# A two-layer streaming encoder step: the delta rule's decay matrices, its rows of exp and all parts of the first output weight are made in the first projection stage and read back from DRAM

## The chip, the core and the metric

The kernel runs on one core of one Trainium2 chip. The metric is the time of one launch on the device in microseconds (us), as the median of the runs; less is better. One further execution was taken by the hardware profiler, and all rows of views below come from that one. The engines are PE (TensorE), ACT (ScalarE), DVE (VectorE), POOL (GpSimd) and SP (SyncE, which here issues most DMAs).

## The reference

2048 prompt tokens and 32 sample tokens (2080 rows of 1024 values, all float32) pass one gated delta layer, a shared K/V projection and one sliding-window attention layer. The change touches the delta layer:

```python
proj = x @ w_in                                  # q, k, v, gate z, and two small columns a, b
qkv  = silu(causal_conv(proj[..., :CONV_DIM]))   # 4 taps; q and k are then l2-normalised
g    = -exp(a_log) * softplus(a_in + dt_bias);  beta = sigmoid(b_in)
# in blocks of c positions, 8 heads:
gcum  = cumsum(g)
decay = exp(where(incl, gcum[:, None] - gcum[None, :], -inf))
lower = where(strict, (k*beta) @ k.T * decay, 0)
u, w  = solve(lower + I, v*beta), solve(lower + I, k*beta*exp(gcum))
intra = q @ k.T * decay
v_new = u - w @ S;   o = (q*exp(gcum)) @ S + intra @ v_new
S     = S * exp(gcum[-1]) + (k*exp(gcum[-1]-gcum)).T @ v_new
out   = (rmsnorm(o) * silu(z)) @ w_out           # then residual and layer norm
```

The kernel uses blocks of 128 positions: 17 tiles, of which tile 0 holds the 32 sample rows (with a state of its own) and tiles 1 to 16 the prompt.

## The kernel before

**Precision.** The large products are made of float32 values split in a high and a low part (`w_hi`, `w_lo`, `act_hi`, `act_lo`), three matmuls each (L77 to L79). The split of a weight is an ACT cast and a POOL or DVE subtraction.

**Order.** The tile framework puts each engine's instructions in an order by an estimate of its own, except where the program switches to an order written out by hand: PE and DVE in the gate stage, and PE, DVE and ACT in the delta loop. SP's queue and POOL's are ordered by the framework throughout, so a DMA need not stand where the program calls for it.

**P1, `P1.qkv`.** The input stays in SBUF as five blocks of 416 rows. First come the small columns, out of which `gates` makes `gcum` for all tiles; it turns each tile's 128 values of 8 heads on PE (L379), copies them on DVE (L381) into one of two row buffers and stores them to the scratch `gcum` from ACT's queue (L382). Then 24 heads (8 of q, 8 of k, 8 of v) follow: PE projects 5 blocks, ACT copies them out of PSUM (L227, six banks in turn), ACT and DVE do the convolution and the SiLU over the whole row of 2083 values (L194, L196, L199, L200), for q and k also the sums of squares (L207 to L210), and SP stores the head (L202). `fetch_weights` (L46) asks for the weight of a later head as soon as its only raw buffer is free. In heads 15 to 22 `split_out_weights` splits the first half of the output weight of the delta layer, a piece of 128 x 512 each, in the buffer that the tanh (`th`) uses, and keeps the parts in the scratch `wo`. After the last head of k, `norms` finishes the factors per token, the bias `ngc` of the decays among them.

**Gate stage.** PE projects the gate z for three of the five blocks; beside it `Ahead` prepares the triangular inverses of tiles 0 and 1.

**Delta loop, `Delta.run`.** Turn i finishes tile i, inverts tile i+1, begins tile i+2 and loads for tile i+3. `decays` makes E, 128 x (8 x 128): DVE adds the mask `nm` to the rows `gb` that were read with broadcast from `gcum` (L542), ACT takes exp with the bias `ngc` (8 times, L547). There is one buffer for E. `lower` multiplies k k^T (PE, L562) by E (DVE, L563) and turns the diagonal blocks into `L` (L572); POOL runs 25 steps of a substitution on it (`chain`: L585 and L588), DVE the rest. `inside` multiplies q k^T (PE, L629) by E (L630). `powers` takes exp of `gb` itself (ACT, L638), and `fade` multiplies k and q by it (DVE, L646). `turn_v` and `turn_k` turn v (PE, L612) and k (L598) on PE. `emit` multiplies the output by the gate and stores it (L800) out of the buffer that the gate was read into; v and z share three buffers of half a tile (L531 loads them). Up to turn 10 (`OPEN` is 11) pieces of the gate projection of the last two blocks fill PE between the steps. Then the left half of SBUF is given to `O1`, the output projection with layer norm, whose tiles fill PE in the last turns. It needs the whole output weight in two parts; `load_part_weights` reads four of the eight pairs from `wo` (L1050, L1051), and four raw weights (L1047), which ACT casts (L1059) and DVE subtracts (L1063), a step at a time in turns 11 to 14.

**Afterwards**: the second layer's projections, the attention and its output projection, which the change does not touch.

Of the kernel before, what the change touches and what calls it, by code (L numbers as in the profile page):

```python
# [26 lines left out]
H = 8  # L27
# [63 lines left out]
def drain(gen):  # L91
    for _ in gen:
        pass


class P1:
# [49 lines left out]
    def qkv(self):  # L146
# [180 lines left out]
def gates(nc, I, T, G, abT, gtmp, one, pt):  # L327
# [135 lines left out]
class Delta:  # L463
# [36 lines left out]
    def constants(self):  # L500
        nc, one = self.nc, self.one
        self.nm = one.tile([128, 128], F32, tag="nm", name="nm")
        nc.sync.dma_start(self.nm[:], self.I["nm"])
        self.tinit = one.tile([128, 32, 8], F32, tag="tinit", name="tinit")
        nc.sync.dma_start(self.tinit[:], self.I["tinit"])
# [5 lines left out]
    def load(self, ch, name, halves=(0, 1)):  # L511
# [25 lines left out]
    def decays(self, ch):  # L537

        nc, V, G = self.nc, self.nc.vector, self.G
        n, ti = ch.n, ch.ti  # L540
        ch.E = self.two.tile([128, 8, 128], F32, tag="E", name="E", bufs=1)
        V.tensor_tensor(out=ch.E[:n, :, :n], in0=ch.gb[:n, :, :n],  # L542
                        in1=self.nm[:n, :n].unsqueeze(1).to_broadcast([n, 8, n]), op=ALU.add)
        yield
        for h in range(8):
            E = ch.E[:n, h, :n]
            nc.scalar.activation(E, E, AF.Exp, bias=G["ngc"][:n, ti, h:h + 1])  # L547
            if h % 4 == 3:
                yield

# [68 lines left out]
    def inside(self, ch):  # L619
# [3 lines left out]
        for q in range(2):  # L623
# [8 lines left out]
            yield  # L632

    def powers(self, ch):

        for hs in (slice(0, 4), slice(4, 8)):
            eg = ch.gb[:, hs, :ch.n]
            self.nc.scalar.activation(eg, eg, AF.Exp)  # L638
        yield

# [162 lines left out]
    def run(self, chunks, S, first, second, side, done):  # L803
# [7 lines left out]
        def go(*gens):  # L811
            for g in gens:
                next(g, None)
# [6 lines left out]
        fill = first.give  # L820
        drain(self.decays(c0))
        side(False)
# [4 lines left out]
        fill(1.0)  # L827
        k, w, g, d, low = self.turn_k(c0), self.turn_v(c0), self.inside(c0), self.decays(c1), self.lower(c1)
        for s, us in ((w, 0.6), (k, 0.6), (w, 0.6), (k, 0.6), (g, 0.6), (g, 0.6), (d, 0.0), (d, 0.0), (d, 1.2), (d, 1.2),
                      (low, 1.2), (low, 1.2)):  # L830
            go(s)
            fill(us)
        drain(self.powers(c0))
        drain(self.fade(c0))
# [6 lines left out]
        drain(self.powers(c1))  # L841
        drain(self.decays(c2))
        self.S, S = S, self.S
# [4 lines left out]
        for i in range(len(chunks) + 1):  # L848
# [32 lines left out]
            go(a, t, a, t, seen, sq)  # L881
            go(gen(self.powers, n2))
            side(0)
# [25 lines left out]
            fill(2 * more + 2 * gate)  # L909
            d = gen(self.decays, n3)  # L910
            go(v)
            fill(gate)
            go(r, g, r, r, r, r, v, r, k, r, d)
            if i > self.OPEN:
# [18 lines left out]
            fill(more)  # L933
            go(v, o, d, d)
            side(1)
# [26 lines left out]
class Ahead(Delta):  # L962
# [13 lines left out]
    def inverses(self, chunks):  # L976

        tmps = []
        for ch in chunks:
            tmp = Chunk(ch.t0, ch.n)  # L980
            own = ch if ch.pool else tmp
            for name in ("gb", "k"):
                self.load(own, name)
            tmp.gb, tmp.k = own.gb, own.k
            tmps.append(tmp)
        yield
        for name in ("q", "v"):
            self.load(chunks[0], name)
        for ch, tmp in zip(chunks, tmps):
            yield from self.decays(tmp)  # L990
# [46 lines left out]

def load_part_weights(nc, pool, stage, src, kept, sub):


    hi, lo = (pool.tile([128, KC, D], F32R, tag=n, name=n) for n in ("wo_hi", "wo_lo"))
    m = kept.shape[1]
    raws = {}

    def load(k):
        raws[k] = stage.tile([128, D], F32, tag="r", name="wo_raw")
        nc.sync.dma_start(raws[k][:], src[k])  # L1047

    def fetch(k, q):
        q.dma_start(hi[:, k, :].bitcast(F32), kept[0, k])  # L1050
        q.dma_start(lo[:, k, :].bitcast(F32), kept[1, k])  # L1051

    yield hi, lo
    load(m)
    load(m + 1)
    fetch(0, nc.sync)
    yield
    for k in range(m, KC):
        nc.scalar.copy(hi[:, k, :], raws[k][:])  # L1059
        if k - m + 1 < m:  # L1060
            fetch(k - m + 1, nc.scalar)
        yield
        sub.tensor_tensor(out=lo[:, k, :], in0=raws[k][:], in1=hi[:, k, :], op=ALU.subtract)  # L1063
        if k + 2 < KC:
            load(k + 2)
        yield
# [37 lines left out]
class OutNorm:  # L1104


    def __init__(self, tc, es, name, side, I, pre, banks, kept):
        self.nc = nc = tc.nc
        self.one = new_pool(tc, es, name + "_one", 1, side=side)
        self.two = new_pool(tc, es, name + "_two", 2, side=side)  # L1110
        self.pp = new_pool(tc, es, name + "_pp", banks, PSUM, side=side)
        self.tabs = None
        self.tables = lambda: ln_tables(nc, self.one, I[pre + "_ln_g"], I[pre + "_ln_b"])
        self.rest = load_part_weights(nc, self.one, self.two, I[pre + "_w_out"], kept, nc.vector)
        self.w = next(self.rest)
# [637 lines left out]
def host_inputs(inp):  # L1753
# [56 lines left out]
    "z": (NTT, 128, 8, 128),  # L1810
    "wo": (2, 4, 128, D),
    "wob": (2, KC, 128, D),
    "gcum": (NTT, 8, 128),
    "o": (NS, 8, 128),
    "g": (NTT, 128, 8, 128),
# [49 lines left out]
```

## Time and profile before

| what | value |
|---|---|
| median of 3 runs | 2196.88 us (2190.58 to 2197.76) |
| the profiled execution | 2196.05 us, its span 2194.3 us |
| busy PE / DVE / ACT / POOL | 2149.0 / 1373.7 / 917.6 / 841.7 us |
| mean granted PE clock | 0.991 |
| moved by DMA | 274.48 MB, mean 125 GB/s |
| P1 and gate stage / delta loop / rest | about 0 to 705 / 705 to 1150 / 1150 to 2194 us |

The rows of the views have this form. In a group: line, engine, operation, output<-input, size, count | busy us in all, mean ns of one | idle us before them and what ended it. In a timeline: start us, length us, engine, line, operation [idle before it <-what ended it]. In a table of stretches: busy us and instructions of PE, of its weight loads, of DVE, ACT and POOL, then the granted PE clock, the share of the DMA engines and GB/s. A "q" behind an engine's name is its sequencer, which issues DMAs.

### The profile page before, as it was taken

The page shows a single profiled execution, that of the slowest core. Times are in us where ns is not written, and L with a number is a line of the kernel's source. Part 1 is how long each engine was busy: PE and PEld are TensorE (multiplying, and loading weights), DVE is VectorE, ACT ScalarE, POOL GpSimd, SP SyncE. Part 2 cuts the span into 40 slices and gives each one's busy share as a digit, 9 for nine tenths or more (in the row PEclk, how much of TensorE's full clock was granted, in tenths as well). Part 3 has the DMA queues.
Part 4 walks back from the last instruction along what each step waited for, and adds up shares of the span by engine and source line. Part 5 has one row for each costly group of instructions (what it writes and reads, how often), then busy time and mean ns, then how long its engine had stood idle before and what let it go on. Part 6 is the DMA issues. An engine that isn't in the chain of part 4 may idle for free.

```text
span 2194.3 us, 36636 instructions
## 1 busy us (share of the span) xinstructions
PE 2149.0 (98%) x13706; PEld 1982.3 (90%) x13706; DVE 1373.7 (63%) x2696; ACT 917.6 (42%) x2303; POOL 841.7 (38%) x1189
## 2 busy tenths in 40 slices
PE   8999999999999999999999999999999999999998
PEld 6999999999999899998888788999999987778885
DVE  3676666754466688888868876135442236668775
ACT  4444344433323677778741213222112235445442
POOL 1422212222211377888820201046441124556564
PEclk9999999999999999999999999999999999999999
DMA  5222222233355344446536754374221288233321
GB/s 198 68 60 79 68 78 68 91 117 97 97 152 156 100 139 148 128 134 216 191 98 198 239 186 154 100 235 167 70 76 67 86 181 267 78 96 97 103 67 53
DMA packets 250674, 274.48 MB, mean 125 GB/s; under 512 B 76112, under 2 KB 195216, under 8 KB 250224
## 3 DMA queue, kind: packets, MB, share of 16 engines
q1 hardware_dynamic: 240528, 256.97, 38.0%
q10 hardware_dynamic: 9968, 15.17, 2.1%
q8 instruction: 108, 1.77, 0.3%
q14 instruction: 70, 0.57, 0.1%
HBM read 168.53 MB, written 103.92 MB: 124 GB/s over the span
## 4 chain that ended last, share of the span: by engine, by line
PE 91%; POOL 3%; DMA 2%; DVE 1%; ACT 1%; issue 1%; ACTq 0%; SPq 0%; DVEq 0%; POOLq 0%
PE ps L77 17%; PE ps L79 17%; PE ps L78 17%; PE po L1089 5%; PE po L1091 5%; PE po L1090 5%; PE ot L1581 4%; PE S L1560 2%; PE tr L1575 2%; POOL Tt L588 1%; POOL tm L585 1%; PE g L562 1%; PE vp L725 1%; PE ks L714 1%; PE op L739 1%; PE gq L629 1%
## 5 line engine op out<-in xcount | busy, mean ns | idle before, releaser
L77 PE MATMUL ps<-act_hi,w_hi 128*128 128x416 f32 x2000 | 706.6, 354 | 4.5 <-ACT w_hi L53 3.2
L79 PE MATMUL ps<-act_hi,w_lo 128*128 128x416 f32 x2000 | 704.9, 353 | 2.0 <-POOL w_lo L54 1.2
L78 PE MATMUL ps<-act_lo,w_hi 128*128 128x416 f32 x2000 | 701.6, 351 | 0.0
L77 PEld LDWEIGHTS ps<-act_hi,w_hi 128*128 128x128 f32 x2000 | 377.0, 189 | 9.1 <-ACT w_hi L53 3.7
L79 PEld LDWEIGHTS ps<-act_hi,w_lo 128*128 128x128 f32 x2000 | 376.1, 188 | 6.8 <-POOL w_lo L54 1.7
L78 PEld LDWEIGHTS ps<-act_lo,w_hi 128*128 128x128 f32 x2000 | 376.5, 188 | 4.7 <-DVE act_lo L69 0.4
L54 POOL TENSOR_TENSOR w_lo<-w_raw,w_hi 128x1024 fp32r<-128x1024 f32 x44 | 117.6, 2673 | 469.2 <-ACT w_hi L53 443.1
L196 DVE SCALAR_TENSOR_TENSOR y<-R,convw,y 128x2083 f32<-128x2083 f32 x72 | 173.7, 2414 | 109.6 <-ACT y L194 74.1
L585 POOL TENSOR_TENSOR tm<-L,Tt 128x60 f32<-128x60 f32 (+19 forms) x373 | 139.4, 374 | 89.9 <-ACT vn L771 49.7
L588 POOL TENSOR_TENSOR Tt<-Tt,tm 128x60 f32<-128x60 f32 (+19 forms) x373 | 157.1, 421 | 29.2
L1568 POOL TENSOR_TENSOR P<-P,sm 128x384 f32<-128x384 f32 (+2 forms) x128 | 100.5, 806 | 172.9 <-DVE sm L1446 104.4
L227 ACT COPY R<-ps 128x416 f32<-128x416 f32 (+1 forms) x144 | 61.2, 448 | 199.0 <-PE ps L79 178.4
L1442 ACT ACTIVATE P<-S,nm 128x192 f32<-128x192 f32 (+3 forms) x260 | 104.6, 418 | 90.0 <-DVE nm L1435 43.3
L1089 PE MATMUL po<-wo_hi,g_hi 128*128 128x512 f32 x256 | 104.0, 406 | 1.8 <-ACT hT L1196 1.8
L1286 POOL TENSOR_TENSOR rs<-rs,sin 128x416 f32<-128x416 f32 x50 | 71.0, 1421 | 78.7 <-DVE rs L1285 72.2
L1091 PE MATMUL po<-wo_hi,g_lo 128*128 128x512 f32 x256 | 100.5, 393 | 0.0
L1090 PE MATMUL po<-wo_lo,g_hi 128*128 128x512 f32 x256 | 100.4, 392 | 0.0
L1581 PE MATMUL ot<-pt,vd 128*128 128x256 f32 x372 | 97.1, 387 | 1.6 <-ACT pt L1577 1.1
L53 ACT CAST w_hi<-w_raw 128x1024 fp32r<-128x1024 f32 x48 | 50.4, 1050 | 114.7 <-PE ps L78 87.3
L1089 PE MATMUL po<-wo,g_hi 128*128 128x512 f32 x224 | 92.9, 415 | 0.0
L1091 PE MATMUL po<-wo,g_lo 128*128 128x512 f32 x224 | 90.0, 402 | 0.0
L1090 PE MATMUL po<-wo,g_hi 128*128 128x512 f32 x224 | 89.8, 401 | 0.0
(306 smaller groups left out, 4041.2 us busy)
## 6 DMA issues: line engine op xcount, KB each, us to landing
w_raw<-in_w_in SPq DMA_DIRECT2D x40, 512.0 KB
w_raw<-in_b_w_in SPq DMA_DIRECT2D x20, 512.0 KB
gb<-s_gcum SPq DMA_DIRECT2D x17, 512.0 KB
k<-s_k SPq DMA_DIRECT2D x17, 512.0 KB
s_bz<-za SPq DMA_DIRECT2D x40, 208.0 KB
s_bq<-ra SPq DMA_DIRECT2D x40, 208.0 KB
s_q<-y SPq DMA_DIRECT2D x8, 1024.0 KB
s_k<-y SPq DMA_DIRECT2D x8, 1024.0 KB
```

What stands on the lines that cost most here:

```text
L54: sub.tensor_tensor(out=lo[:], in0=raw[:], in1=hi[:], op=ALU.subtract)
L77: nc.tensor.matmul(ps, hi[:, k, :], xh[:, k, :], start=(k == 0), stop=False)
L78: nc.tensor.matmul(ps, hi[:, k, :], xl[:, k, :], start=False, stop=False)
L79: nc.tensor.matmul(ps, lo[:, k, :], xh[:, k, :], start=False, stop=(k == KC - 1))
L196: nc.vector.scalar_tensor_tensor(out=y[:], in0=R[:, j:j + W], scalar=self.convw[:, i, j:j + 1], in1=y[:], op0=ALU.mult, op1=ALU.add)
L585: P.tensor_tensor(out=tm[:n, i0 - k:, :w], in0=L[:n, i0:, j:j + 1].to_broadcast(sh), in1=Tt[:n, j:j + 1, :w].to_broadcast(sh), op=ALU.mult)
L588: P.tensor_tensor(out=Tt[:n, i0:, :w], in0=Tt[:n, i0:, :w], in1=tm[:n, i0 - k:, :w], op=ALU.subtract)
L1089: nc.tensor.matmul(ps[:n], ghi[:, k, :n], w[0][:, k, cs], start=a, stop=False)
L1090: nc.tensor.matmul(ps[:n], ghi[:, k, :n], w[1][:, k, cs], start=False, stop=False)
L1091: nc.tensor.matmul(ps[:n], glo[:, k, :n], w[0][:, k, cs], start=False, stop=z)
L1442: nc.scalar.activation(P[u], src, AF.Exp, bias=nm[:, u:u + 1], scale=1.0, accum_out=sm[:, u:u + 1])
L1581: nc.tensor.matmul(ot[:, p], self.vd[:, kc0 + j, p, :], pt[:, 2 * j:2 * j + 2, :], start=(j == 0), stop=(j == nj - 1))
```

## The change

- `P1.decays` is new. In heads 16 to 23 of P1 it makes E for all 17 tiles in halves of four heads: SP reads `gcum` with broadcast, DVE adds the mask, ACT takes exp, and ACT's queue stores the half to a new scratch `E`. Its three buffers take the places of `parts`, `sel` and `gtmp`, and the mask that of `triu`.
- `gates` also takes exp of each row, and stores both rows (`gcum`, `grow`); there is one row buffer for the two instead of two buffers.
- `split_out_weights` runs in heads 7 to 22 and splits the whole output weight; `load_whole_weights` reads all sixteen parts on SP's queue.
- In the delta loop and in `Ahead`, `decays` and `powers` are gone; E and the rows of exp are loaded by SP.

```diff
+        matrices = self.decays()
         wo = split_out_weights(nc, one, "th", I["a_w_out"], T["wo"])
...
-            if 15 <= i < 23:
+            if 7 <= i < 23:
                 next(wo)
+            if i >= 16:
+                for _ in range(5 if i < 18 else 4):
+                    next(matrices)
...
+    def decays(self):
+        nc, G, T = self.nc, self.G, self.T
+        nm = self.one.tile([128, 128], F32, tag="triu", name="nm")
+        nc.sync.dma_start(nm[:], self.I["nm"])
+        todo = [(t, q) for t in (NTT - 1, *range(NTT - 1)) for q in range(2)]
+        def load(m):
+            t, q = todo[m]
+            n, hs = min(128, NT - t * 128), slice(q * 4, q * 4 + 4)
+            E = self.one.tile([128, 4, 128], F32, tag=("parts", "sel", "gtmp")[m % 3], name="E")
+            nc.sync.dma_start(E[:, :, :n], T["gcum"][t, hs, :n].partition_broadcast(128))
+            return E, t, n, hs
+        ahead = [load(0), load(1)]
+        for m in range(len(todo)):
+            E, t, n, hs = ahead.pop(0)
+            if m + 2 < len(todo):
+                ahead.append(load(m + 2))
+            nc.vector.tensor_tensor(out=E[:n, :, :n], in0=E[:n, :, :n],
+                                    in1=nm[:n, :n].unsqueeze(1).to_broadcast([n, 4, n]), op=ALU.add)
+            for j in range(4):
+                h = hs.start + j
+                nc.scalar.activation(E[:n, j, :n], E[:n, j, :n], AF.Exp, bias=G["ngc"][:n, t, h:h + 1])
+            nc.scalar.dma_start(T["E"][t, :n, hs, :n], E[:n, :, :n])
+            yield
...
-        row = one.tile([H, 128], F32, tag="g_row", name="g_row", bufs=2)
-        V.tensor_copy(row[:, :n], tp[:H, :n])
-        nc.scalar.dma_start(T["gcum"][t, :, :n], row[:, :n])
+        row = one.tile([H, 2, 128], F32, tag="g_row", name="g_row", bufs=1)
+        V.tensor_copy(row[:, 0, :n], tp[:H, :n])
+        nc.scalar.activation(row[:, 1, :n], tp[:H, :n], AF.Exp)
+        nc.scalar.dma_start(T["gcum"][t, :, :n], row[:, 0, :n])
+        nc.scalar.dma_start(T["grow"][t, :, :n], row[:, 1, :n])
...
         if name == "gb":
-            nc.sync.dma_start(ch.gb[:, :, :n], T["gcum"][ti, :, :n].partition_broadcast(128))
+            nc.sync.dma_start(ch.gb[:, :, :n], T["grow"][ti, :, :n].partition_broadcast(128))
+        if name == "E":
+            ch.E = self.two.tile([128, 8, 128], F32, tag="E", name="E", bufs=1)
+            nc.sync.dma_start(ch.E[:n, :, :n], T["E"][ti, :n, :, :n])
...
-            go(r, g, r, r, r, r, v, r, k, r, d)
+            go(r, g, r, r, r, r, v, r, k, r)
+            if n3:
+                self.load(n3, "E")
...
-def load_part_weights(nc, pool, stage, src, kept, sub):
+def load_whole_weights(nc, pool, kept):
     hi, lo = (pool.tile([128, KC, D], F32R, tag=n, name=n) for n in ("wo_hi", "wo_lo"))
...
     yield hi, lo
+    for k in range(KC):
+        nc.sync.dma_start(hi[:, k, :].bitcast(F32), kept[0, k])
+        nc.sync.dma_start(lo[:, k, :].bitcast(F32), kept[1, k])
         yield
```

More of the change, by code (lines that the diff above doesn't have):

```diff
@@ L532, in load @@
         if name == "gb":
-            nc.sync.dma_start(ch.gb[:, :, :n], T["gcum"][ti, :, :n].partition_broadcast(128))
+            nc.sync.dma_start(ch.gb[:, :, :n], T["grow"][ti, :, :n].partition_broadcast(128))
+        if name == "E":
+            ch.E = self.two.tile([128, 8, 128], F32, tag="E", name="E", bufs=1)
+            nc.sync.dma_start(ch.E[:n, :, :n], T["E"][ti, :n, :, :n])
         if name == "k":
             nc.sync.dma_start(ch.k[:, :, :n], T["k"][ti, :, :, :n])
[L537 to L549, printed above, removed]
     def lower(self, ch):
@@ L632, in inside @@
             yield
[L634 to L639, printed above, removed]
     def fade(self, ch):
@@ L820, in run @@
         fill = first.give
-        drain(self.decays(c0))
+        self.load(c0, "E")
         side(False)
@@ L827, in run @@
         fill(1.0)
-        k, w, g, d, low = self.turn_k(c0), self.turn_v(c0), self.inside(c0), self.decays(c1), self.lower(c1)
-        for s, us in ((w, 0.6), (k, 0.6), (w, 0.6), (k, 0.6), (g, 0.6), (g, 0.6), (d, 0.0), (d, 0.0), (d, 1.2), (d, 1.2),
-                      (low, 1.2), (low, 1.2)):
+        k, w, g, low = self.turn_k(c0), self.turn_v(c0), self.inside(c0), self.lower(c1)
+        for s, us in ((w, 0.6), (k, 0.6), (w, 0.6), (k, 0.6), (g, 0.6), (g, 0.6)):
             go(s)
             fill(us)
-        drain(self.powers(c0))
+        self.load(c1, "E")
+        fill(2.4)
+        for s, us in ((low, 1.2), (low, 1.2)):
+            go(s)
+            fill(us)
         drain(self.fade(c0))
@@ L840, in run @@
             fill(us)
-        drain(self.powers(c1))
-        drain(self.decays(c2))
+        self.load(c2, "E")
         self.S, S = S, self.S
@@ L981, in inverses @@
             own = ch if ch.pool else tmp
-            for name in ("gb", "k"):
-                self.load(own, name)
-            tmp.gb, tmp.k = own.gb, own.k
+            self.load(own, "k")
+            tmp.k = own.k
             tmps.append(tmp)
         yield
-        for name in ("q", "v"):
+        for name in ("gb", "q", "v"):
             self.load(chunks[0], name)
         for ch, tmp in zip(chunks, tmps):
-            yield from self.decays(tmp)
+            self.load(tmp, "E")
+            yield
+            yield
+            yield
             yield from self.lower(tmp)
@@ L1035, in split_out_weights @@
             yield
-def load_part_weights(nc, pool, stage, src, kept, sub):
+def load_whole_weights(nc, pool, kept):
     hi, lo = (pool.tile([128, KC, D], F32R, tag=n, name=n) for n in ("wo_hi", "wo_lo"))
[L1042 to L1051, printed above, removed]
-    yield hi, lo
[L1054 to L1065, printed above, removed]
+    yield hi, lo
+    for k in range(KC):
+        nc.sync.dma_start(hi[:, k, :].bitcast(F32), kept[0, k])
+        nc.sync.dma_start(lo[:, k, :].bitcast(F32), kept[1, k])
         yield
@@ L1113, in __init__ @@
         self.tables = lambda: ln_tables(nc, self.one, I[pre + "_ln_g"], I[pre + "_ln_b"])
-        self.rest = load_part_weights(nc, self.one, self.two, I[pre + "_w_out"], kept, nc.vector)
+        self.rest = load_whole_weights(nc, self.one, kept)
         self.w = next(self.rest)
```

10 lines of the change are left out of this document (4 added, 6 removed).

## The prediction

> **What bounds the kernel now.** I read the head of the page first, then the busy time by stretches, then the chain of waits in the stretches where TensorE (PE) is not full, and last the DMA queue of SyncE (SP) there. The page:
>
> ```profile
> span 2194.3 us, 36636 instructions
> PE 2149.0 (98%) x13706; PEld 1982.3 (90%) x13706; DVE 1373.7 (63%) x2696; ACT 917.6 (42%) x2303; POOL 841.7 (38%) x1189
> ```
>
> PE is idle for 2194.3 - 2149.0 = 45.3 us in all, and the change gives PE no instruction and takes none away. So a gain can come only out of those 45 us, and a loss only by new idle time of PE. The stretches (busy us, then granted clock, DMA share, GB/s) say where the 45 us are:
>
> ```profile
> 300.00:400.00 100.00, 100.00 (x532) 99.32 (x531) 61.69 (x27) 42.62 (x51) 20.67 (x21) 1.00 0.26 78
> 900.00:1000.00 100.00, 100.00 (x1119) 95.65 (x1118) 84.67 (x202) 77.31 (x246) 78.99 (x202) 1.00 0.42 136
> 1000.00:1100.00 100.00, 90.79 (x1068) 85.94 (x1068) 85.13 (x207) 81.64 (x254) 83.27 (x210) 0.97 0.58 198
> ```
>
> The first projection stage (P1, to about 600) and the first eleven turns of the delta loop (to about 1005, where gate projections fill the gaps) keep PE full: what the change does to DVE, ACT and POOL there is worth nothing as long as it stays hidden. Only 1000 to 1100, turns 11 to 14 without that filler, has idle PE: 9.2 us. The chain of waits runs there through POOL's substitution chain (L585, L588), one chain per turn:
>
> ```profile
> 1040.30 0.28 POOL tm L585
> ...
> 1064.40 0.28 POOL tm L585
> ```
>
> 24.1 us from the start of the chain of tile 14 to that of tile 15. So these turns, and these alone, go by POOL.
>
> **The change, part by part.** (1) *Decays and powers leave the loop.* Their groups before:
>
> ```profile
> L547 ACT ACTIVATE E<-E,t_ngc 128x128 f32<-128x128 f32 (+1 forms) x152 | 45.1, 381 | 11.6 <-DVE E L542 11.6
> L542 DVE TENSOR_TENSOR E<-gb,nm 128x1024 f32<-128x1024 f32 (+1 forms) x19 | 22.8, 1198 | 0.0
> L638 ACT ACTIVATE gb<-gb 128x512 f32<-128x512 f32 (+1 forms) x34 | 18.8, 601 | 0.0
> ```
>
> That is 1.2 us of DVE and (45.1 + 18.8) / 17 = 3.8 us of ACT a tile, and with it the splitting of four weight parts. On DVE and ACT this is covered by PE or POOL. But in the POOL-bound turns it comes back through POOL itself, which slows beside these two DVE additions:
>
> ```profile
> 1049.92 1.38 DVE L542 TENSOR_TENSOR E<-gb,nm 128x1024 f32<-128x1024 f32 x1
> 1050.29 1.17 POOL L585 TENSOR_TENSOR tm<-L,Tt 128x72 f32<-128x72 f32 x1
> 1051.22 1.32 DVE L1063 TENSOR_TENSOR wo_lo<-wo_raw,wo_hi 128x1024 fp32r<-128x1024 f32 x1
> 1051.54 1.20 POOL L588 TENSOR_TENSOR Tt<-Tt,tm 128x72 f32<-128x72 f32 x1
> 1052.81 0.31 POOL L585 TENSOR_TENSOR tm<-L,Tt 128x68 f32<-128x68 f32 x1
> 1053.20 0.35 POOL L588 TENSOR_TENSOR Tt<-Tt,tm 128x68 f32<-128x68 f32 x1
> ```
>
> 1.17 against 0.31, and 1.20 against 0.35: 1.7 us a chain. Both additions go, or in turn 14 two of the second kind. Over the chains of tiles 14, 15 and 16 the gain is 3 x 1.7 = **-5.1 us** (0 if something else than POOL is late by then, -6 with the ACT copies of the weights, also gone).
>
> (2) *All 16 halves of the output weight are loaded, none is made in the loop.* This is the part that decides. The diff calls for one pair a step from turn 11 on, but SP's order is made by the scheduler, and in the built program all sixteen loads stand on SP's queue before the stores and loads of turn 11, with only one v, one q and one g load between them. What stands there now:
>
> ```profile
> 1004.74 0.81 SPq L1047 DMA_DIRECT2D wo_raw<-in_a_w_out  x2
> 1005.64 0.38 SPq L1050 DMA_DIRECT2D wo_hi<-s_wo  x1
> 1006.06 0.43 SPq L1051 DMA_DIRECT2D wo_lo<-s_wo  x1
> ...
> 1013.73 0.92 SPq L800 DMA_DIRECT2D s_g<-z  x2
> ...
> 1020.13 0.32 SPq L531 DMA_DIRECT2D v<-s_v  x1
> ```
>
> Four loads of 512 KB now, sixteen after, and behind them in the changed order: the store of the gated output (s_g), gb, the two norm tables, two rows of x, q, and only then the second half of v of tile 13, then k and E of tile 14. That half of v takes the buffer (three, shared by v and z) out of which s_g is stored, so it is not even issued until s_g has landed; the wait is there already and is short now:
>
> ```profile
> SPq L531 <- DMA s_g<-z: 13.5, 27, 2.7
> ```
>
> The sizes (KB each) and the rate at which the queue drains when full:
>
> ```profile
> wo_hi<-s_wo SPq DMA_DIRECT2D x1, 512.0 KB
> g<-s_g SPq DMA_DIRECT2D x16, 512.0 KB
> v<-s_v SPq DMA_DIRECT2D x32, 256.0 KB
> ...
> 1005.00:1010.00 5.00, 5.00 (x59) 4.70 (x55) 4.01 (x8) 4.96 (x16) 4.53 (x7) 1.00 0.87 282
> 1010.00:1015.00 5.00, 5.00 (x47) 5.00 (x46) 4.01 (x7) 4.63 (x13) 4.22 (x11) 1.00 1.05 390
> 1015.00:1020.00 5.00, 4.78 (x43) 4.59 (x43) 5.00 (x16) 3.95 (x20) 3.68 (x13) 1.00 1.00 354
> ```
>
> Up to s_g the queue has to move E 0.52, weights 8.39, v and q 0.52, g 0.52, s_g 0.52: 10.5 MB, at 354 to 390 GB/s 27 to 30 us from 1005, so to 1032 to 1035. Then come gb, tables, rows, q and v: 3.1 MB, 8 to 9 us. So v lands between 1040 and 1044; I take 1042. Who waits for it, and what stands behind:
>
> ```profile
> 1027.66 0.66 PE L612 MATMUL vtr<-ident,v 128*128 128x128 f32 x4
> 1030.65 2.05 PE L562 MATMUL g<-k 128*128 128x128 f32 x16
> ...
> 1036.94 2.00 DVE L572 STREAM_TRANSPOSE L<-nb 128x1024 f32<-128x1024 f32 x1
> ```
>
> PE turns that v at 1027.7 and takes its orders in sequence, so it stands still for 1042 - 1027.7 = 14.3 us (12 to 16). Behind it wait the four transposes of k, the last product of the inversion and, 3.0 us later, L562 of tile 14; from there it is 8.3 us (1038.94 - 1030.65) until L is turned and POOL's chain of tile 14 can start: 1042 + 3.0 + 8.3 = 1053.3 instead of 1040.3, **+13.0 us**. PE will also come out of the pause at a lower clock, as after shorter ones now:
>
> ```profile
> 1032.54 1.95 PE L725 MATMUL vp<-vn,u 128*128 128x128 f32 x16
> ...
> 1104.64 3.66 PE L725 MATMUL vp<-vn,u 128*128 128x128 f32 x16 [0.91 <-ACT u L705]
> ```
>
> The same 16 products took 1.88 times as long, so the 3.0 us before L562 become up to 5.6: **+2 us** (0 to 2.6). The Trainium skill, page "TensorE: Matmul & The Clock Gate", section "What's actually happening", says that one idle window of about 3.4 us puts the clock to half and that about 3.4 us of work bring it back; by that rule the pause costs the whole 3.0 us once more, and the sum would be 1 us higher; the trace's 3.66 against 1.95 agrees with the half.
>
> (3) *E is loaded instead of made, in each turn.* The one buffer is free after the second product with E, and the next use is the first one of the following turn:
>
> ```profile
> 1048.05 0.69 DVE L630 TENSOR_TENSOR at<-gq,E 128x512 f32<-128x512 f32 x1 [0.15 <-PE gq L629]
> ...
> 1056.43 0.69 DVE L563 TENSOR_TENSOR npr<-g,E 128x512 f32<-128x512 f32 x1 [0.36 <-ACT E L547]
> ...
> 1211.19 5.10 DMA r<-in_x
> ```
>
> From 1048.74 to 1056.43 are 7.7 us; a load of 512 KB that was waited for cost 5.1 us of the chain at a busy time. With SP's own 0.3 to 0.4 us it lands some 2 us early: 0, and if that cover is gone, what the landing lacks, in each turn. SP also waits there until the product is done, with only v and q loads of the next turn behind it. The 3.8 us of ACT no longer stand before npr, but PE is full: -1 us over eleven turns, at most -3.
>
> (4) *P1 makes 34 half matrices* (four heads by 128 columns): 34 x 1.198 / 2 = 20 us of DVE, about 45 us of ACT, 34 loads and 34 stores over some 180 us, and from head 7 on eight more weight steps through the buffer that the tanh uses. DVE has 38 us in a hundred free there, ACT 57. PE needs from them the copies out of six PSUM banks and the next weights, which are asked for a whole head ahead:
>
> ```profile
> POOL w_lo L54 <- DMA s_gcum<-g_row: 16.3, 1, 16.3
> ...
> 1785.78 0.46 PE L77 MATMUL ps<-act_hi,w_hi 128*128 128x416 f32 x1 [3.22 <-ACT w_hi L53]
> ```
>
> POOL's splitting of a weight has waited 16.3 us for one small store in P1, and still PE's longest wait for a weight's cast, 3.2 us, lies at 1786, far behind P1. So I take 0, with +6 for the upper end: the 17 rows of gates now go through one buffer with two stores each instead of two buffers with one, DVE and ACT wait for the landing each time, and PE's turning of the next row can wait for them.
>
> **Sum**, against the profiled execution's 2196.05 us (0.8 us under the median of the runs, 2196.88): -5.1 + 13.0 + 2 - 1 + 1 (a little of the 6) = +9.9, so **2206 us**. Its own range: the least, -6 + 10.3 - 3 = +1, 2197; the most, 0 + 15.3 + 2.6 + 6 = +24, 2220 if the POOL gain is lost too.
>
> **Rivals.** *A, the weights are hidden and the gain stays.* v comes before 1028: the loads of the weights are spread over the turns, as the diff has them, or small ones pass big ones in the queue. It decides as soon as v lands within 3 us of now. Against it: one queue, and 390 GB/s at a share of 1.05 now, which can't be raised threefold. For it: PE has no recorded wait for v now, though 2 MB stand before one of its halves. Time: 2196 - 5.1 - 1 = 2190, the side that isn't slower.
>
> *B, P1 stalls.* ACT holds groups of four or eight exps between the copies out of PSUM, and SP three loads of E ahead of each weight fetch; when one of them is late by more than a head's slack (about 20 us), PE waits. Price: two heads that lose 8 us each, 2206 + 16 = 2222. For it: thirty-four loops of load, add, exps and store through three buffers; against it: the free shares above.
>
> *C, E is late in every turn.* The load lands over 7.7 us after its buffer is free, because z stores and w_raw of 512 KB lie before it. One us late in each of 14 turns: 2206 + 14 = 2220. Against it: DMA share 0.42 in 900 to 1000.
>
> *D, the weight halves are simply not slower to load than to make and POOL isn't the bound any more*, so that neither +13 nor -5 shows: 2196.
>
> **How the numbers follow.** Main case 0.57, A 0.16, B 0.13, C 0.08, D 0.06. No change means within 0.3%, 6.6 us, about what a measurement of this kernel can tell. Slower: 0.7 of the main case, B and C: 0.61; faster: somewhat over half of A and a little of the main case: 0.12; the rest, 0.27, is the same. Range 2190 to 2223: it leaves out the lower half of A and the tails of B and C.
>
> **What would show it.** Right: DMA share near 1 from 1005 to about 1042; PE waiting over 10 us at the turning of v (line of L612) in turn 11, followed by half clock; POOL's chains under 23 us afterwards and without the 1.2 us instructions beside E's addition; no idle PE before 1000. Wrong: v there on time, PE idle in P1, or products npr waiting for the load of E turn after turn.

## The result, and the profile after

The changed kernel takes 2215.65 us (median of 4; 2210.15 to 2218.2) where the kernel before takes 2195.80 beside it: a ratio of 1.0091, 95% interval 1.0063 to 1.0118. It is slower, by some 20 us of the medians. Its profiled execution is its fastest one, 2210.15 us with a span of 2208.3, 14.0 us over the span before. What follows accounts for these 14.0 us; the other 6 or so lie in executions of which no trace was kept, and the last part comes back to them.

The head of its page:

```profile
span 2208.3 us, 36932 instructions
PE 2145.5 (97%) x13706; PEld 1975.8 (89%) x13706; DVE 1378.3 (62%) x2707; ACT 899.7 (41%) x2274; POOL 832.7 (38%) x1197
```

The same 13706 products, and 3.5 us less busy time, for 17.5 us more of idle PE. Busy time holds products at half clock too, so it can shrink with the same work. To see where it arises, PE's weight loads (13706 in both) were put in order of time in both traces and the start of each compared with that of the same number before. This table of delays in us, taken around the time in the kernel before that heads the column, is used for all runs below:

| kernel | 540 | 610 | 1000 | 1030 | 1060 | 1150 | 2180 |
|---|---|---|---|---|---|---|---|
| changed | 0.1 | 11.5 | 7.0 | 21.5 | 19.5 | 10.9 | 14.2 |
| e1, weights on ACT's queue | -0.1 | 10.2 | 10.2 | 10.2 | 9.2 | 3.8 | 3.7 |
| e2, weights alone | 0.0 | 0.0 | 0.0 | 13.9 | 12.1 | 6.6 | 6.1 |
| e3, decays alone | 0.3 | 14.6 | 14.5 | 14.5 | 13.6 | 11.5 | 12.9 |
| e5, in effect the changed kernel again | 0.6 | 14.0 | 9.5 | 25.1 | 25.6 | 16.8 | 17.3 |
| f1, four buffers | 0.8 | 9.5 | 9.4 | 24.0 | 22.2 | 17.2 | 16.8 |
| f2 = f1 and ACT's queue | 0.3 | 2.4 | 2.3 | 2.3 | 5.5 | -1.1 | -2.8 |
| f3, two buffers | 0.1 | 33.2 | 33.2 | 48.7 | 49.0 | 40.3 | 37.8 |
| f4 = e2 on ACT's queue | 0.1 | 0.1 | 0.1 | 0.1 | 0.3 | -6.8 | -7.4 |
| g1 = f2, weights in heads 0 to 15 | 7.6 | 7.6 | 7.5 | 7.5 | 6.5 | 1.3 | 4.8 |
| g2, twelve of sixteen on SP | 0.1 | 11.4 | 11.4 | 21.9 | 20.2 | 12.4 | 13.0 |
| h1 = f2, weights in heads 3 to 18 | 0.1 | 0.6 | -0.8 | -0.8 | -1.8 | -7.0 | -3.3 |

Four steps stand in the first row. The delta loop loses 14.5 us between 1026 and 1030, as predicted; this is called the loss at v below. The first stage (P1) loses 11.5 us between 570 and 610, of which the prediction had 1; this is the loss in P1. Between 700 and 750 the kernel gains 4.5 us, for which the last section has the reason as far as it is known. And between 1060 and 1150 the loop gives back 8.6.

The loss at v, in the waits of PE and the chain of waits of the changed kernel:

```profile
PE vtr L632 <- DMA v<-s_v: 13.2, 1, 13.2
```

```profile
1012.18 8.11 DMA wo_lo<-s_wo
1020.31 8.97 DMA wo_hi<-s_wo
1029.34 9.89 DMA s_g<-z
1039.29 8.41 DMA v<-s_v
1047.84 1.09 PE vtr L632 x4
...
1052.19 1.98 PE g L582 x16
```

SP's queue in the same stretch, issue by issue, and PE by stretches (the last three numbers of a row are the granted clock, where 1.00 is the full one, the DMA share and GB/s):

```profile
1010.79 0.38 SPq L1060 DMA_DIRECT2D wo_hi<-s_wo  x1
...
1028.03 0.32 SPq L1061 DMA_DIRECT2D wo_lo<-s_wo  x1
1029.34 1.60 SPq L813 DMA_DIRECT2D s_g<-z  x2
...
1039.29 0.33 SPq L562 DMA_DIRECT2D v<-s_v  x1
```

```profile
1020.00:1030.00 10.00, 8.91 (x105) 8.49 (x102) 9.73 (x28) 6.96 (x29) 7.14 (x23) 1.00 1.03 402
1030.00:1040.00 10.00, 4.62 (x76) 4.06 (x76) 4.82 (x16) 4.67 (x12) 8.28 (x22) 0.85 1.03 408
1040.00:1050.00 10.00, 2.16 (x10) 2.19 (x11) 0.00 (x0) 1.04 (x4) 3.68 (x12) 0.50 1.00 390
```

Sixteen loads pass, then the store of the gated output, and v can be issued only when that store has landed. While the weights pass, the queue is full (share 1.00 to 1.03) and PE runs out of work.

The loss in P1, PE by stretches (busy, clock, DMA share, GB/s) in the last heads of P1, and the waits of all engines from 420 to 620:

```profile
570.00:580.00 10.00, 9.68 (x52) 1.00 0.57 181
580.00:590.00 10.00, 5.56 (x22) 0.82 0.71 200
590.00:600.00 10.00, 10.00 (x47) 0.84 0.35 135
600.00:610.00 10.00, 8.33 (x45) 1.00 0.59 167
```

```profile
DVE E L239 <- DMA E<-s_gcum: 59.0, 18, 10.2
...
PE ps L77 <- ACT R L258: 3.0, 3, 2.3
```

PE waits only 3.0 us for ACT's copies out of PSUM (L258) here, and 2.1 and 1.7 us for w_lo, but then also runs at a lower clock. DVE waits 59 us for loads of E. Why, the chain of waits between 540 and 612 shows:

```profile
551.80 7.73 DMA E<-s_gcum
...
559.73 0.70 DVE E L239
...
561.35 0.42 ACT E L243 x2
561.76 4.87 DMA s_E<-E
566.77 3.64 DMA E<-s_gcum
...
585.08 6.13 DMA E<-s_gcum
...
592.03 2.31 DVE y L200
...
602.00 1.06 ACT w_hi L309
603.13 2.36 POOL w_lo L301
```

One buffer's round: load, addition, exps, store, and the next load of that buffer waits for the store. Three such rounds run side by side. Behind the last load stands the convolution of the last head (L200), and behind that the split of the next weight (L309, L301), for which PE waits. SP's queue issued the fifth load at 463.20 and the last, the 34th, at 585.08:

```profile
463.20 0.32 SPq L231 DMA_DIRECT2D E<-s_gcum  x1
```

```profile
585.08 0.42 SPq L231 DMA_DIRECT2D E<-s_gcum  x1
```

That is 121.9 / 29 = 4.2 us a matrix, so 12.6 us a round.

### The profile page after: what moved, and what is told of

The parts are those of the page before. It is cut to its first block, busy times and chain, and to the rows that moved or that the text cites. A ratio compares the mean times of both kernels' runs of the same rounds, so it can differ in the third digit from the quotient of the medians.

```text
span 2208.3 us, 36932 instructions
## 1 busy us (share of the span) xinstructions
PE 2145.5 (97%) x13706; PEld 1975.8 (89%) x13706; DVE 1378.3 (62%) x2707; ACT 899.7 (41%) x2274; POOL 832.7 (38%) x1197
## 4 chain that ended last, share of the span: by engine, by line
PE 83%; DMA 6%; DVE 4%; ACT 3%; POOL 2%; issue 1%; ACTq 0%; SPq 0%; DVEq 0%; POOLq 0%
PE ps L77 15%; PE ps L79 15%; PE ps L78 15%; PE po L1085 5%; PE po L1087 5%; PE po L1086 5%; PE ot L1577 4%; PE S L1556 2%; PE tr L1571 2%; DMA E<-s_gcum 2%; PE g L582 1%; PE vp L738 1%; PE op L752 1%; DMA s_E<-E 1%; PE op L756 1%
## 5 line engine op out<-in xcount | busy, mean ns | idle before, releaser
L79 PEld LDWEIGHTS ps<-act_hi,w_lo 128*128 128x128 f32 x2000 | 376.7, 188 | 11.5 <-POOL w_lo L54 3.9
L200 DVE SCALAR_TENSOR_TENSOR y<-R,convw,y 128x2083 f32<-128x2083 f32 x72 | 181.8, 2526 | 38.6 <-POOL convo L194 22.4
L605 POOL TENSOR_TENSOR tm<-L,Tt 128x60 f32<-128x60 f32 (+19 forms) x373 | 128.3, 344 | 110.6 <-PE op L752 42.9
L608 POOL TENSOR_TENSOR Tt<-Tt,tm 128x60 f32<-128x60 f32 (+19 forms) x373 | 151.1, 405 | 29.2
L258 ACT COPY R<-ps 128x416 f32<-128x416 f32 (+1 forms) x144 | 60.7, 445 | 123.9 <-PE ps L79 106.0
L53 ACT CAST w_hi<-w_raw 128x1024 fp32r<-128x1024 f32 x48 | 50.4, 1049 | 109.7 <-PE ps L78 80.0
```

The lines of the kernel that those rows point to most:

```text
L79: nc.tensor.matmul(ps, lo[:, k, :], xh[:, k, :], start=False, stop=(k == KC - 1))
L200: nc.vector.scalar_tensor_tensor(out=y[:], in0=R[:, j:j + W], scalar=self.convw[:, i, j:j + 1], in1=y[:], op0=ALU.mult, op1=ALU.add)
L605: P.tensor_tensor(out=tm[:n, i0 - k:, :w], in0=L[:n, i0:, j:j + 1].to_broadcast(sh), in1=Tt[:n, j:j + 1, :w].to_broadcast(sh), op=ALU.mult)
L608: P.tensor_tensor(out=Tt[:n, i0:, :w], in0=Tt[:n, i0:, :w], in1=tm[:n, i0 - k:, :w], op=ALU.subtract)
```

## Experiments

### e1, e2, e3: the two halves of the change, and the order on SP's queue

e1 is the changed kernel with one edit, in load_whole_weights:

```diff
-        nc.sync.dma_start(hi[:, k, :].bitcast(F32), kept[0, k])
-        nc.sync.dma_start(lo[:, k, :].bitcast(F32), kept[1, k])
+        nc.scalar.dma_start(hi[:, k, :].bitcast(F32), kept[0, k])
+        nc.scalar.dma_start(lo[:, k, :].bitcast(F32), kept[1, k])
```

> The changed kernel with its sixteen loads of weight halves issued on ACT's queue, whose order is the program's: one to four pairs a turn over turns 11 to 14 instead of all sixteen ahead of turn 11's loads on SP's queue. Theory (the order on SP's queue costs 13 to 14 us): the wait of PE for v at its turning (13.2 us in the changed kernel) is under 1 us, the half clock after it is gone, and the time is 12 to 14 us under the changed kernel, 2202 to 2204, since the loss of 7 us in the first stage stays. Rival (8.4 MB have to pass in these turns, whichever queue they use): something of turns 11 to 14 waits as long as before, 2211 to 2216.

Measured: 2203.85 us, 1.0042 (1.0028 to 1.0057) of before, so 11.8 us under the changed kernel. PE has no wait for v any more, and the delay goes through 1030 unchanged at 10.2. The same sixteen loads are made; a stretch of e1:

```profile
1000.00:1100.00 100.00, 92.89 (x1069) 87.85 (x1067) 82.02 (x215) 68.12 (x227) 79.42 (x217) 1.00 0.76 253
```

The changed kernel moves 254 GB/s over the same 100 us with PE busy for 81.39 of them. So the loss was the order, not the amount. Two things changed in the order: the loads stand on another queue than v, and they are issued a pair at a time, some 11 us apart from 1047 on, instead of sixteen within 18 us. Which of the two does it was not separated. The Trainium skill, page "DMA: Bandwidth & Descriptors", section "Issuing engines are not separate DMA queues", says that DMAs of all issuing engines run on the same 16 DMA engines, and that issuing from several saves only the sequencer's time. In e1, with loads on both queues, no 2.5 us slice of this stretch moves more than 413 GB/s, against 419 in the changed kernel with all of them on SP's queue, which agrees with the first. The second does not hold for this kernel's time, of which 11.8 us went.

e2 is the kernel before with the weights' half of the change alone (heads 7 to 22, load_whole_weights on SP's queue).

> The kernel before with the weights' half of the change alone: sixteen half steps in heads 7 to 22, whole halves loaded on SP's queue; decays and powers stay in the loop. Theory (two separate losses): no idle PE in the first stage, PE waits 11 to 14 us for v in turn 11, and the POOL chains lose only the slow instruction beside the weight's subtraction: 9 to 12 us over the kernel before, 2205 to 2208. Rival (the additional weight steps fill up the first stage): PE idle between 560 and 610 here as well, 2212 to 2216.

Measured: 2203.17 us, 1.0041 (1.0027 to 1.0055), 2 us below the range of the expectation. No delay at 610, and the wait is there:

```profile
PE vtr L612 <- DMA v<-s_v: 12.3, 1, 12.3
```

So the loss in P1 does not come from the added weight steps alone.

e3 is the changed kernel with the weights as before.

> The changed kernel with the weights as before (four weight parts split in heads 15 to 22, the rest made in the loop): the decay matrices and rows of exp alone. Theory: PE loses 5 to 8 us between 560 and 610, no long wait for v, and the POOL chains of tiles 14 to 16 are 1.2 us faster each: 2 to 5 us over the kernel before, 2198 to 2201. Rival (the matrices in the first stage cost nothing without the weight steps, as I predicted): 2190 to 2193.

Measured: 2206.37 us, 1.0056 (1.0038 to 1.0073). No wait for v, and a delay of 14.6 us at 610: the decay matrices alone make the whole loss in P1, more than the 5 to 8 expected, and the loop returns only 3.0 us of it by 1150. The time lies 5 us above the expected range. My prediction's "0" for this part is refuted, and so is the rival's time.

### e5, f1, f3: what makes the first stage late

e5 calls for the half matrices between the steps of the convolution:

```diff
-            if i >= 16:
-                for _ in range(5 if i < 18 else 4):
-                    next(matrices)
...
             for j in range(1, 4):
                 nc.vector.scalar_tensor_tensor(...)
+                if i >= 16:
+                    next(matrices)
+            if i >= 16:
+                for _ in range(2 if i < 18 else 1):
+                    next(matrices)
```

> The changed kernel with the four or five half matrices of a head put between the four steps of its convolution and after them instead of all ahead of it, so that the convolution does not stand behind all their loads on DVE. Theory (DVE waits in order for loads of E, 59 us in the last heads, and this makes the convolution and PSUM's copies late): the idle PE between 560 and 610 falls under 2 us, 5 to 7 us under the changed kernel, 2208 to 2211. Rival (ACT's exps, or the rows of the gates through one buffer, are the reason): no change, 2214 to 2217.

Measured: 2217.33 us, 1.0109 (1.0087 to 1.0131), 14.0 us of delay at 610. But the edit did not do what it was to do. The framework orders P1, and in the traces of e5 and of the changed kernel the instructions of every engine and the DMAs of every queue follow one another in the same order, with the same shapes: e5 is the changed kernel once more. In both, the additions of E already stand between the steps of the convolution, not all ahead of it (on DVE from 483 us of the changed kernel: E, y, y, E, y, E, E), so the expectation started from a wrong premise, and whether their place matters was not tested. What e5 tells is how far two measurements of one program lie apart: 2215.65 and 2217.33 us, and in the traces 11.5 and 14.0 us of delay at 610. In e5, too, the fifth to the 34th load of E take 587.49 - 463.91 = 123.6 us, 4.3 a matrix. That the turnover of the buffers makes P1 late became the next theory, and two kernels change the number of buffers, with the loads ahead that go with it, and nothing else. f1 has four (gtmp holds two) with three loads ahead, f3 has two with one ahead:

```diff
+        g = self.one.tile([128, 2, 4, 128], F32, tag="gtmp", name="E")
+        ring = [self.one.tile([128, 4, 128], F32, tag=tag, name="E")[:] for tag in ("parts", "sel")]
+        ring += [g[:, 0], g[:, 1]]
...
-            E = self.one.tile([128, 4, 128], F32, tag=("parts", "sel", "gtmp")[m % 3], name="E")
+            E = ring[m % 4]
```

> The changed kernel with four buffers instead of three for the half matrices of E in the first stage (gtmp holds two of them) and three loads ahead instead of two. Theory (the turnover of three buffers, load, addition, exps and store one after the other, some 12.6 us a round and so 4.2 us a matrix, is what makes the convolution late): 3.2 us a matrix, so 34 matrices take 107 us instead of 143, and PE's delay by the end of the first stage falls from 11.5 us to under 4: 2207 to 2210. Rival (DVE and ACT themselves are full in the last heads): the delay stays at 9 to 12 us, 2214 to 2217.

> The changed kernel with two buffers instead of three for the half matrices in the first stage and one load ahead. Theory (turnover of the buffers): 6.3 us a matrix, 34 take 214 us instead of 143, and PE loses 50 to 70 us more in the first stage: 2265 to 2290. Rival (the work of DVE and ACT sets the loss): the work is the same, within 5 us of the changed kernel, 2211 to 2221.

Measured: f1 2212.04 us, 1.0063 (1.0042 to 1.0084); f3 2236.03 us, 1.0182 (1.0155 to 1.0210). The fifth and the last load of E on SP's queue, of f1 and of f3:

```profile
467.42 0.32 SPq L234 DMA_DIRECT2D E<-s_gcum  x1
```

```profile
562.36 0.32 SPq L234 DMA_DIRECT2D E<-s_gcum  x1
```

```profile
466.41 1.71 SPq L231 DMA_DIRECT2D E<-s_gcum  x1
```

```profile
628.37 0.32 SPq L231 DMA_DIRECT2D E<-s_gcum  x1
```

| buffers | 29 loads, us | us a matrix | us a round | delay at 610, us |
|---|---|---|---|---|
| 2 | 162.0 | 5.6 | 11.2 | 33.2 |
| 3 | 121.9 | 4.2 | 12.6 | 11.5 |
| 4 | 94.9 | 3.3 | 13.1 | 9.5 |

The round stays at 11 to 13 us while the work is the same, so the time of the matrices is round over buffers: that the turnover sets their pace is shown. PE's delay follows it in direction but not in size: f3 was expected to lose 50 to 70 us more and lost 22, and f1 kept 9.5 where under 4 was expected. f1's time missed its expectation by 2 us as well. The medians say the same: the fourth buffer takes 3.6 us off the changed kernel (f1), and 8.2 off e1 (f2 below). In f3 the price is one wait at the end of the first stage, where DVE, still at the matrices, comes late to the gate projections' PSUM (L272):

```profile
PE ps L77 <- DVE z L272: 31.0, 1, 31.0
```

f2 below runs the same first stage as f1 and has a delay of 2.4. In f1 6.7 of the 9.5 arise between 590 and 600, where PE waits 2.5 us for the next weight's cast (w_hi, L312) and the clock then falls to half; in f2 that wait does not show. So some of the loss in P1 is a short wait made longer by the clock, and it comes and goes with a few us of the transfers. The weight steps have a share in it that was not separated: from 420 to 620 ACT of the changed kernel also waits 18.4 us for loads of output weight pieces and 6.8 us, ahead of such a piece, for a store of E. e3, which has the same steps in these heads, has 14.6 at 610; g1 and h1 below, with four buffers and the steps moved ahead, lose 0.0 and 0.4 us from 540 to 610; three buffers with the steps moved were not run.

### g2: are the bytes ahead of v its price?

```diff
+        q = nc.sync if k < 6 else nc.scalar
-        nc.sync.dma_start(hi[:, k, :].bitcast(F32), kept[0, k])
-        nc.sync.dma_start(lo[:, k, :].bitcast(F32), kept[1, k])
+        q.dma_start(hi[:, k, :].bitcast(F32), kept[0, k])
+        q.dma_start(lo[:, k, :].bitcast(F32), kept[1, k])
```

> The changed kernel with twelve of the sixteen loads of weight halves on SP's queue as before and four on ACT's queue in turn 14. Theory (v waits for the bytes ahead of it on SP's queue, at 390 to 408 GB/s): 2.1 MB less are 5.3 us, so PE's wait for v falls from 13.2 to about 8 us (7 to 9), time 2209 to 2213. Rival (v waits for the number of loads in flight or for one late transfer, not for bytes): the wait stays at 12 to 14 us, or goes below 3.

Measured: 2210.09 us, 1.0074 (1.0049 to 1.0099), and

```profile
PE vtr L632 <- DMA v<-s_v: 8.5, 1, 8.5
```

4.7 us less for 2.1 MB less, where 5.3 were worked out: the wait falls with what is left ahead of v, nearly at the rate of the queue. All these loads have one size, so bytes and number of loads can't be told apart here; only the rival as it was put, no change or under 3 us, is out.

### f2, f4, g1, h1: is there a version that gains?

f2 is f1 with the weight halves on ACT's queue. f4 is the kernel before with whole weight halves on ACT's queue and nothing else of the change.

> The changed kernel with four buffers as in the run before and with the weight halves loaded on ACT's queue as well. Theory (the two losses are separate, and 6 us of gain in turns 11 to 16 are left when both are gone): 6 to 8 us under e1's 2203.9, so 2194 to 2198 if the first stage keeps a delay of 3 us, and 2188 to 2191, under the kernel before, if it keeps none. Rival (the first stage stays late whatever the buffers): 2202 to 2205.

> The kernel before with whole weight halves, split in heads 7 to 22 and loaded on ACT's queue over turns 11 to 14; decays and powers stay in the loop. Theory: no loss in the first stage and none at the turning of v, and the weights' share of the gain in the POOL chains (1.2 us for each of two or three): 2190 to 2193, 1 to 4 us under the kernel before. Rival (the loads themselves, on any queue, cost turns 11 to 14 what the second kernel of this series lost, 9 us): 2200 to 2204.

Measured: f2 2195.70 us, 1.0006 (0.9993 to 1.0018); f4 2191.34 us, 0.9976 (0.9965 to 0.9988). f4 beats both kernels. f2 loses neither 14 nor 11 us, and gains nothing that its interval can tell: its row of the table holds another 3.2 us between 1030 and 1060, where PE is full but at half clock (busy, clock, DMA share, GB/s):

```profile
1050.00:1060.00 10.00, 10.00 (x92) 0.53 0.67 215
```

g1 and h1 are f2 with the weight's half steps in other heads, one line each:

```diff
-            if 7 <= i < 23:
+            if i < 16:          # g1;  h1: if 3 <= i < 19:
                 next(wo)
```

> The run with four buffers and ACT's queue (f2), with the sixteen half steps of the weight in heads 0 to 15 instead of 7 to 22, so that they are over when the matrices begin. Theory (what is left of the loss in the first stage, 2.4 us of delay in f2's trace, comes from sharing the last heads with the weight steps): delay at the end of the first stage under 1 us, 2191 to 2194, 2 to 4 us under f2. Rival (the matrices alone make it): 2195 to 2198 as f2.

> As g1 with the sixteen half steps in heads 3 to 18: behind the gates of the first heads, where g1 lost 7 us at once, and over before most of the matrices. Theory: delay under 1 us at the end of the first stage; turns 11 to 16 give back 6 to 7 us as in e1, g1 and f4: 2188 to 2191, 5 to 8 us under the kernel before and at or under f4's 2191.3. Rival (the trip of the decay matrices through scratch costs later stages what the loop gains, so that f4 stays the best): 2192 to 2196.

Measured: g1 2200.36 us, 1.0024 (1.0011 to 1.0038); h1 2192.52 us, 0.9989 (0.9979 to 0.9999). g1 gave what it was to tell, no delay arises between 540 and 610, but its time missed both expectations: it loses 7 us between 100 and 120. Its rows on ACT show that the first stage has the same trap at its start:

```profile
96.13 1.95 ACT L203 ACTIVATE th<-y 128x2083 f32<-128x2083 f32 x1 [14.78 <-DMA s_wo<-wo_parts]
...
108.43 0.62 ACT L1052 CAST wo_parts<-wo_parts 128x512 fp32r<-128x512 f32 x1 [4.56 <-DMA wo_parts<-in_a_w_out]
108.95 2.19 ACT L261 COPY R<-ps 128x416 f32<-128x416 f32 x6
```

The tanh shares a buffer with the weight parts and waits for their store, then a cast waits for their load, and six copies out of PSUM stand behind both on ACT. h1 avoids both ends: 0.6 us of delay at 610, -7.0 at 1150, as its theory had it. Its time lies in the rival's range, though, because 3.7 us are lost after 1150, where f4 gains 0.6; g1 loses 3.5 there, e1 and f2 nothing. Much of that difference arises near 1786, where PE waits 4.0 us in h1 and 3.2 in the kernel before for the cast of a weight (L53), with a half clock behind it, and 0.9 us in f4 without one. Whether the matrices' way through scratch costs the later stages the rest is left open.

From 1000 to 1150 the loop gains as much in f4 (6.9), which keeps all decays and powers in the loop, as in h1 (6.2), but not for the same reasons. POOL's chains of tiles 14 to 16 took 71.3 us together before. They take 67.4 in f4 and 68.2 in e2 (weights alone), 69.5 in e3 (decays alone), and 66.4 in the changed kernel and 65.8 in h1 (both): each half shortens them, and both together most. The rest is the clock. Rows of the kernel before, of f4 and of h1 behind the last chain (busy, clock, DMA share, GB/s):

```profile
1130.00:1140.00 10.00, 10.00 (x55) 0.73 0.03 11
```

```profile
1130.00:1140.00 10.00, 10.00 (x81) 1.00 0.24 96
```

```profile
1120.00:1130.00 10.00, 10.00 (x93) 0.66 0.15 52
```

The kernel before runs at half clock from 1128.5 to 1135.3 us, h1 does as it passes the same work, and f4 does not. So f4 gains 2.9 us between 1112, where the last chain of the kernel before is over, and 1150, and h1 0.3.

## Why the prediction was right or wrong

The forecast was 2206.0 us, range 2190 to 2223, for 2215.65; slower was given 0.61. The time lies in the range and 9.6 us over the forecast, 4 us over it by the profiled execution.

*What bounds the kernel now*: right. The turns after 1005 were the ones to look at, but P1 was not as safe as "stays hidden" assumed, and "only out of those 45 us" left out what PE loses while it is busy, at half clock: 4.5 us between 700 and 750 and 3.1 after 1112 came back that way.

*(2), the weights on SP's queue*: right in its mechanism and nearly in its numbers, once the 7.0 us that the kernel is late by then are added. s_g was to land at 1032 to 1035, which is 1039 to 1042 with these 7.0 us, and did at 1039.2; v at 1042, so 1049, and did at 1047.7. PE waited 13.2 us for 14.3. POOL's chain of tile 14 was to start 13.0 us later, and 2 for the clock:

```profile
1060.40 0.26 POOL L605 TENSOR_TENSOR tm<-L,Tt 128x31 f32<-128x31 f32 x1 [15.79 <-ACT vn L784]
...
1082.76 0.28 POOL L605 TENSOR_TENSOR tm<-L,Tt 128x31 f32<-128x31 f32 x1
```

1060.4 - 1040.3 - 7.0 = 13.1. The half clock is there (0.50 from 1040 to 1050), but from v to L582 it took 4.35 us for 3.0, so the clock cost some 1.4 and not 2. e1, e2 and g2 confirm this step by itself. In the range of the sum, 10.3 and 15.3 do not follow from a wait of 12 to 16 us, which gives 10.7 and 14.7; nothing hangs on it.

*(1), decays and powers leave the loop*: the term is right, the reason only in part. The chains of tiles 14 to 16 took 24.0, 24.1 and 23.2 us before and take 22.3, 22.5 and 21.6: -4.9 for -5.1. The delay falls by 5.5 us from 1060 to 1112, while chains run, but by 8.6 until 1150. What the sum lacked is the clock: the other 3.1 us lie where the kernel before ran at half clock from 1128.5 to 1135.3 (its row above), and the changed kernel at 1.00 from 1060 to 1150:

```profile
1060.00:1150.00 90.00, 82.25 (x931) 1.00 0.38 118
```

All runs bear this out. Those that have no half clock on the work that the kernel before does from 1112 to 1150 gain 2.9 to 3.2 us there (changed, e5, f2, f3, f4, g2), those with 6.8 us of it 0.0 to 0.3 (e1, e3, g1, h1), e2, with 3.4 us of it, 1.8, and f1, with 10.2 us of it, loses 0.9.

The products quoted in the prediction at 3.66 us take less in f4:

```profile
1102.38 2.05 PE L725 MATMUL vp<-vn,u 128*128 128x128 f32 x16 [0.91 <-ACT u L705]
```

after the same wait of 0.91 us.

*(3), E loaded in each turn*: right that it costs nothing. E is issued as its buffer comes free and nothing waits for it:

```profile
1067.58 0.69 DVE L650 TENSOR_TENSOR at<-gq,E 128x512 f32<-128x512 f32 x1 [0.15 <-PE gq L649]
1075.26 0.69 DVE L583 TENSOR_TENSOR npr<-g,E 128x512 f32<-128x512 f32 x1 [0.94 <-PE g L582]
```

7.0 us lie between the one use and the next, for 7.7 before, and the later one waits for PE; no instruction of the loop is recorded as waiting for a load of E. The -1 us from ACT's relief did not show: the delay is 7.0 at 750 and at 1000. Rival C is wrong.

*(4), P1 makes 34 half matrices*: this is the step that failed. "So I take 0, with +6" stood for 11.5 us of delay at 610. Free shares of DVE and ACT were the wrong measure: the matrices do not fill these engines, they pass through three buffers, each bound for 12.6 us, mostly by two transfers, so that 34 x 4.2 = 143 us go by until the convolution of the last head, in line behind the last of them on DVE, is done and the next weight can be split. The +6 had a wrong reason too: the gates' rows through one buffer cost nothing, the delay at 540 is 0.1. Rival B, "P1 stalls", named the loops of load, add, exps and store through three buffers and got 0.13; two heads at 8 us was its price. It happened together with the main case, in kind if not at the place it named: SP's loads and ACT's exps were late, and PE paid at the end of P1.

*The sum* of the profiled execution, against -5.1 + 13.0 + 2 - 1 + 1 = 9.9: first stage +11.5, then -4.5 between 700 and 750 (below), +14.5 at v, -10.6 from there to 1150, and +3.3 after: 14.2. The forecast had only the loss at v and the gain of the chains of these terms. That it came within 4 us of the profiled execution is partly luck: it missed 10.5 us in P1, and 4.5 between 700 and 750 and 3.1 after 1112, which it had not forecast, made up for most of that. The last 3.3 arise where the change touches nothing; over the other runs the same stretch gives -2.5 to +3.7, part of it near 1786 as said above, and the rest was not followed. The other executions of the changed kernel take 3.7 to 8 us more than the profiled one. Their recorded mean clocks are 0.988 to 0.989, its own is 0.991; 0.002 to 0.003 of 2208 us are 4.4 to 6.6 us, an estimate by which most of that is the clock. Where in these executions it fell is not on record.

## What to carry to other kernels

Work moved into a stage with free engines is priced by the round of its buffers (load, work, store, over the number of buffers), not by the engines' shares; a buffer more or fewer tells it. A burst of loads on one queue is paid by the first small load behind it that is waited for, here 13.2 us behind sixteen loads and 8.5 behind twelve; issuing them on a queue whose order is the program's, some each turn, took the whole wait away. Where a framework orders the instructions, look in the trace whether an edit moved anything: e5 moved nothing. Undo each half of a change alone before believing its reason: here the half that kept its gain was the weights', on ACT's queue, 2191.3 us against 2194.0.

## What was not expected of the hardware

The clock falls to half in stretches in which PE is recorded as full, and with the same work not in each kernel. In the kernel before, PE by stretches (busy, clock, DMA share, GB/s), with a gap of 1.3 us in all in the first of them:

```profile
715.00:720.00 5.00, 3.66 (x24) 1.00 0.21 54
...
740.00:745.00 5.00, 5.00 (x19) 0.50 0.33 105
```

and in the changed kernel, the same gap 10 us later and no fall:

```profile
725.00:730.00 5.00, 3.69 (x23) 1.00 0.02 4
...
740.00:745.00 5.00, 5.00 (x46) 1.00 0.49 151
```

This is the step from 11.5 to 7.0 in the table. The gap is hardly the reason: PE is full for some 18 us between it and the fall, which comes at 736.0. Just ahead of the fall stand the products of tile 0, which use 32 of the 128 rows or columns of the array, in the kernel before and, without a fall, in the changed one:

```profile
728.09 1.94 PE L714 MATMUL ks<-Sp,k 128*32 128x128 f32 x16
```

```profile
739.49 1.94 PE L727 MATMUL ks<-Sp,k 128*32 128x128 f32 x16
```

In all eleven traces that have the fall it comes 7.5 to 10.1 us after the first of these products; the changed kernel and e5, the same program, escape it. That these small products are the reason is likely, but no run shows it. The Trainium skill, page "TensorE: Matmul & The Clock Gate", section "What's actually happening", has the clock set by how busy PE was in a window of some 3.4 us that runs freely. The half clock lasts 3.4, 6.8, 10.2 us or a higher multiple of 3.4 each time in these traces, but for the one that the end of the execution cuts off, which agrees with such a window, and so does it that the same work meets it in one kernel and not in another. That a window with PE recorded as full counts as idle is not in that section. For a kernel such as this one it means that differences of 4 to 5 us between two profiled executions need no cause in the code.
